# The last feature pair of each FFN chunk: third operand difference from the first, split in two steps, with priority in the schedule

## The chip, the cores and the metric

One core of a Trainium2 chip. The metric is the device time of one execution in microseconds (us). Several executions are timed, and the median is compared.

## The reference

One step of a decoder layer on 512 new prompt tokens and 8 sample tokens (520 columns), model width 1024: half a SwiGLU FFN, a mixer (causal pooling beside a Mamba-2 state-space scan), half a second SwiGLU FFN, a final norm. The change touches the two FFNs alone:

```python
def _swiglu(x, wg, wu, wd):
    return (jax.nn.silu(x @ wg) * (x @ wu)) @ wd

h = h + 0.5 * _swiglu(_rms_norm(h, ffn1_norm[l]), ffn1_w_gate[l], ffn1_w_up[l], ffn1_w_down[l])
```

The inner width is 2816, which is 22 tiles of 128, called features here. All inputs are float32.

## The kernel before

**Arithmetic.** A float32 product is emulated: each operand is split into a high part (a rounded cast, ScalarE) and a low part (operand minus high part, VectorE), and `mm3` (L122 to L127) issues three matmuls, high by high (L123), high weight by low activation (L126), low weight by high activation (L127), each 128x128 by 128x260. 260 is half of the 520 tokens.

**Seven products instead of eight.** Gate and up weights of a feature (or two output tiles `d`, `d + 1` of the down projection), two halves of the contraction and two token halves make a 2x2 by 2x2 block product. The class `Ffn` does it with seven products of blocks (`product`, L412 to L439), whose operands are sums and differences of blocks. For the down projection the activation side comes from *pairs* of features: `gx` is the first one's output and `go` the second one's, each with two token halves, and `xd` are four differences of them. The seven operands of a pair lie as slots of one tile `gt` (high parts 0 to 6, low parts 7 to 13): slot 0 is `gx0`, 1 `go0`, 2 `go1`, 3 to 6 `xd0` to `xd3`. Products use them so: product 1 slot 0, product 2 slot 1, product 5 slot 3, product 6 slot 5, product 3 slot 2, product 7 slot 4, product 4 slot 6.

**PSUM.** Products 1, 6, 7 and 4 accumulate one after another in one bank `A`; 5 and then 3 in the second half of `BE`; 2 in its first half. After products 1, 6, 7 and 5 ScalarE copies the bank out (`ac`, L437) before the next product may go on in it. So product 6 waits for the copy of product 1, product 7 for that of 6, product 4 for that of 7, and product 3 for that of 5.

**Weights.** `load` splits for each step the weight blocks `whi/wlo_..a` (products 1 and 2), `shi/slo_..c` (made from the sum `s1`; products 7 and 5), `shi/slo_..d` (from `s2`; products 6 and 3) and `whi/wlo_..b` (product 4). The high parts are ScalarE casts (L107). The low parts come from VectorE (L114), or for half of `wlo` from an ScalarE negation (L110) and an accumulating DMA that GpSimd issues (L111). The tag `shi` has two buffers, `whi` three.

**Loops.** The features go in chunks of 6, 6, 6 and 4; the first three chunks are paired. `rest` runs for each paired chunk the steps of its features, then the step of the next chunk's first feature, then four down steps `(c, d)`, d = 0, 2, 4, 6. In the profile `A1d`, `BE1d`, `shi_1d_0c` and so on are those of ffn1's down steps (2d: ffn2), here of chunk 0. A `step` opens product 1, then flushes the pending step before it (its product 4 and `close`), then runs products 5, 6, 3, 7, 2 and the element-wise `gates`. Each of a down step's products reads three pairs (three times three matmuls); the chunk's last pair is finished last: its second feature's half 1 is known after `gates`, half 0 only after that feature's product 4, in `close`. `g_split` makes the operands: for the last pair in two calls, one in `gates` (`late=False`) and one in `close` (`late=True`).

**What sets the order.** The source order above is only the start: a list scheduler with a timeline model places the instructions of all engines, moving matmuls of different steps past one another where data and buffers allow it, by priorities that follow the source. `tc.high_priority()` around a block raises the priority of its instructions. On the chip each engine takes its instructions in the order that results.

The places that the change touches are the boundaries "last feature of a paired chunk, first feature of the next, first down step": feature 5 with 6, 11 with 12, 17 with 18, in both FFNs, six in all.

Of the kernel before, what the change touches and what calls it, by code (L numbers as in the profile page):

```python
# [11 lines left out]
AF = mybir.ActivationFunctionType  # L12
ALU = mybir.AluOpType
# [8 lines left out]
HB = NT // 2  # L22
# [12 lines left out]
PAIRED = 3  # L35
# [26 lines left out]
def tile_trunk_step(ctx: ExitStack, tc: tile.TileContext, ins: dict, outs: dict):  # L62
    nc = tc.nc
# [144 lines left out]
    class Ffn:  # L208
# [42 lines left out]
        def g_split(self, f, late=None):  # L251
            role = self.role(f)
            if role == "plain" and late is not False:
                self.g_plain(f, self.out[f])
            if role != "second":
                return
            last = f == self.chunks[self.chunk[f]][-1]
            if not last and late is False:
                return
            gx, go = self.gx, self.out[f]  # L260
            if not last or late is not True:
                self.gt[f] = (self.gp.tile([P, 14, HB], F32R, tag="gt", bufs=3, name=f"gt{self.i}_{f}"),
                              self.gp.tile([P, 4, HB], F32, tag="xd", name=f"gd{self.i}_{f}"))
            t, xd = self.gt[f]

            def low(x, q):
                hi, lo = t[:, 0:7][:, q], t[:, 7:14][:, q]
                nc.scalar.copy(hi, x)
                nc.vector.tensor_tensor(out=lo, in0=x, in1=hi.bitcast(F32), op=ALU.subtract)

            if not last or late is not True:
                nc.vector.tensor_tensor(out=xd[:, 0], in0=gx[:, 0], in1=gx[:, 1], op=ALU.subtract)
                nc.vector.tensor_tensor(out=xd[:, 1], in0=go[:, 1], in1=gx[:, 1], op=ALU.subtract)
                nc.vector.scalar_tensor_tensor(out=xd[:, 2], in0=xd[:, 1], scalar=-1.0, in1=gx[:, 0], op0=ALU.mult,
                                               op1=ALU.subtract)
                low(gx[:, 0], 0)
                if last:
                    low(go[:, 1], 2)
                    low(xd[:, 0:3], slice(3, 6))
            if last and late is False:  # L280
                return
            nc.vector.scalar_tensor_tensor(out=xd[:, 3], in0=xd[:, 2], scalar=-1.0, in1=go[:, 0], op0=ALU.mult,
                                           op1=ALU.subtract)
            if last:
                low(go[:, 0], 1)
                low(xd[:, 3], 6)
            else:
                low(go, slice(1, 3))
                low(xd, slice(3, 7))
# [154 lines left out]
        def gates(self, k):  # L444
            n = f"{self.i}_{k}" if not isinstance(k, tuple) else f"{self.i}d{k[1]}_{k[0]}"
            r = self.nx[3].rearrange("p (b t) -> p b t", b=2)
            tg = self.tg[k] = self.wx.tile([P, 2, HB], F32, tag="tg", bufs=2, name=f"tg{n}")
            a, c = self.ac[k]
            nc.vector.tensor_tensor(out=tg, in0=self.BE[k][:, :, :HB], in1=a, op=ALU.add)  # L449
            if isinstance(k, tuple):  # L450
                hd, hn = h[:, k[1]], h[:, k[1] + 1, HALVES[1]]
                nc.vector.tensor_tensor(out=hd, in0=hd, in1=tg.rearrange("p b t -> p (b t)"), op=ALU.add)
                nc.vector.tensor_tensor(out=hn, in0=hn, in1=c[:, 0], op=ALU.subtract)
                return
            nc.vector.tensor_tensor(out=tg, in0=tg, in1=r, op=ALU.mult)  # L455
            nc.scalar.activation(out=tg, in_=tg, func=AF.Silu)  # L456
            self.g_homes(k)
            nc.vector.tensor_tensor(out=tg, in0=tg, in1=r, op=ALU.mult)  # L458
            self.up(k, 1, c[:, 0])
            self.g_split(k, False)  # L460

        def up(self, k, b, u):
            out, tg = self.out[k][:, b], self.tg[k][:, b]
# [2 lines left out]
        def close(self, k):  # L466
            if isinstance(k, tuple):
                hn = h[:, k[1] + 1, HALVES[0]]
                nc.vector.tensor_tensor(out=hn, in0=hn, in1=self.A[k][:, :HB], op=ALU.subtract)
                return  # L470
            self.up(k, 0, self.A[k][:, :HB])
            self.g_split(k, True)

        def scales(self):
            return rstds(self.nx, f"f{self.i}")
# [821 lines left out]
```

## Time and profile before

| | |
|---|---|
| median of 3 executions | 982.45 us (980.93 to 982.63) |
| the profiled execution | 982.63 us, its span 980.9 us |
| mean granted TensorE clock | 0.995 |
| matmuls (PE) busy | 950.7 us, 97% |
| VectorE (DVE) busy | 876.8 us, 89% |
| ScalarE (ACT) busy | 682.9 us, 70% |
| GpSimd (POOL) busy | 220.3 us, 22% |

The span is from the first to the last instruction of the profiled execution; 1.7 us of its time lie outside. Busy times are sums over an engine's instructions as the profiler recorded them. A matmul is listed with some 0.28 us from start to end, but matmuls are pipelined: what a stretch costs is read from start to start. Where a row ends in brackets, the engine was idle for that long before the instruction, and the name is what released it.

### The profile page before, as it was taken

Reading aid. Unit: us, or ns where it says so; the run is one execution under the profiler, and the core shown is the slowest. Engines: PE = TensorE matmul, PEld = TensorE weight load, DVE = VectorE, ACT = ScalarE, POOL = GpSimd, SP = SyncE. Lnnn points to the kernel's source line nnn. Section 1 sums busy time; section 2 is a strip of 40 time slices with the busy share of each in tenths; the row PEclk is TensorE's granted clock in tenths of the full one; section 3 lists DMA queues with packets and bytes.
Section 4 is the critical chain, followed back from the end, with each engine's and each line's share of the span. In section 5 each row is a group of like instructions: output and inputs, shape, how many; then the busy total and the mean of one; then the engine's idle time right before and its main releaser. Section 6 shows DMA issues by size and latency. Waiting matters only on the chain.

```text
span 980.9 us, 20300 instructions
## 1 busy us (share of the span) xinstructions
PE 950.7 (97%) x7660; PEld 928.2 (95%) x7660; DVE 876.8 (89%) x1624; ACT 682.9 (70%) x1267; POOL 220.3 (22%) x321
## 2 busy tenths in 40 slices
PE   7999999999999999999999999999999999999996
PEld 6999999999999999999899998899999999999995
DVE  7999899989988698688979987999999998999976
ACT  8777777777777565694754335678888888887864
POOL 0111211221121000167311000113343233233300
PEclk9999999999999999999999999999999999999998
DMA  7666766576566242363334333357687768767732
GB/s 244 179 145 141 184 141 161 128 183 165 120 158 162 78 159 87 103 210 92 120 98 164 100 110 94 106 149 165 165 215 184 183 157 223 191 155 190 190 91 88
DMA packets 63858, 146.51 MB, mean 149 GB/s; under 512 B 9288, under 2 KB 22536, under 8 KB 63760
## 3 DMA queue, kind: packets, MB, share of 16 engines
q1 hardware_dynamic: 41168, 103.78, 33.3%
q0 software_dynamic: 22592, 41.43, 23.3%
q8 instruction: 60, 0.98, 0.4%
q14 instruction: 38, 0.31, 0.1%
HBM read 137.85 MB, written 7.34 MB: 148 GB/s over the span
## 4 chain that ended last, share of the span: by engine, by line
PE 82%; DVE 9%; ACT 3%; DMA 3%; issue 2%; SPq 0%; POOL 0%; DVEq 0%; ACTq 0%
PE A L127 7%; PE A L123 7%; PE A L126 7%; PE BE L123 6%; PE BE L126 6%; PE BE L127 6%; PE P L315 3%; PE wo L123 2%; PE wo L127 2%; PE wo L126 2%; PE inz L123 2%; PE inz L126 2%; PE inz L127 2%; PE A2d L126 2%; PE A2d L127 2%
## 5 line engine op out<-in xcount | busy, mean ns | idle before, releaser
L437 ACT COPY ac<-A 128x260 f32<-128x260 f32 x123 | 45.3, 370 | 19.5 <-PE A L127 19.2
L385 DVE TENSOR_TENSOR s<-raw 128x1024 f32<-128x1024 f32 x41 | 49.9, 1217 | 2.0 <-DMA raw<-in_w2gu 0.9
L107 ACT CAST whi_wo<-raw_wo 128x1024 fp32r<-128x1024 f32 x12 | 12.6, 1046 | 36.8 <-issue 10.3
L1005 POOL DMA_DIRECT2D out_nss<-hs x32 | 20.8, 649 | 76.8 <-DVE hs L1023 76.8
L126 PE MATMUL wo<-catg,whi_wo 128*128 128x260 f32 x128 | 36.4, 285 | 1.3 <-DVE catg L1154 1.3
L123 PE MATMUL wo<-catg,whi_wo 128*128 128x260 f32 x128 | 37.3, 292 | 0.3 <-DVE h L1123 0.3
L123 PE MATMUL inz<-xh_mx,whi_inz 128*128 128x260 f32 x128 | 37.5, 293 | 0.0
L315 PE MATMUL P<-xg_f,raw 128*128 128x260 f32 x128 | 31.7, 401 | 5.5 <-ACT sq_f L163 5.5
L126 PE MATMUL inz<-xl_mx,whi_inz 128*128 128x260 f32 x128 | 36.9, 288 | 0.0
L127 PE MATMUL inz<-xh_mx,wlo_inz 128*128 128x260 f32 x128 | 36.9, 288 | 0.0
L123 PE MATMUL inx<-xh_mx,whi_inx 128*128 128x260 f32 x128 | 36.4, 285 | 0.0
L127 PE MATMUL wo<-catg,wlo_wo 128*128 128x260 f32 x128 | 36.4, 285 | 0.0
L127 PE MATMUL inx<-xh_mx,wlo_inx 128*128 128x260 f32 x128 | 36.2, 283 | 0.0
L126 PE MATMUL inx<-xl_mx,whi_inx 128*128 128x260 f32 x128 | 36.1, 282 | 0.0
L315 PEld LDWEIGHTS P<-xg_f,raw 128*128 128x128 f32 x128 | 25.2, 201 | 9.3 <-ACT xg_f L192 5.5
L449 DVE TENSOR_TENSOR tg<-BE,ac 128x520 f32<-128x520 f32 x41 | 28.4, 693 | 5.5 <-PE BE L127 5.5
L869 DVE SCALAR_TENSOR_TENSOR A<-U,h,A 128x544 f32<-128x544 f32 x36 | 29.0, 805 | 4.0 <-ACT A L867 3.2
L458 DVE TENSOR_TENSOR tg<-tg,r_f 128x520 f32<-128x520 f32 x41 | 28.4, 694 | 1.2 <-ACT tg L456 1.0
L455 DVE TENSOR_TENSOR tg<-tg,r_f 128x520 f32<-128x520 f32 x41 | 28.4, 693 | 0.1
L386 DVE TENSOR_TENSOR s<-s,raw 128x512 f32<-128x512 f32 x41 | 28.0, 683 | 0.0
L387 DVE TENSOR_TENSOR s<-s,raw 128x512 f32<-128x512 f32 x41 | 28.0, 682 | 0.0
L456 ACT ACTIVATE tg<-tg 128x520 f32<-128x520 f32 x41 | 26.1, 638 | 2.5 <-DVE tg L455 2.2
(1798 smaller groups left out, 4788.2 us busy)
## 6 DMA issues: line engine op xcount, KB each, us to landing
raw<-in_w2gu SPq DMA_DIRECT2D x44, 512.0 KB, 4.9
raw<-in_w1gu SPq DMA_DIRECT2D x42, 512.0 KB, 4.7
raw_1d<-in_w1d SPq DMA_DIRECT2D x24, 384.0 KB, 4.0
raw_2d<-in_w2d SPq DMA_DIRECT2D x24, 384.0 KB, 4.2
raw_wo<-in_w_out SPq DMA_DIRECT2D x12, 512.0 KB, 4.3
ab<-scr_acs SPq DMA_DIRECT2D x8, 512.0 KB, 4.1
h<-in_state_ssm SPq DMA_DIRECT2D x16, 256.0 KB, 3.7
raw_inz<-in_w_in SPq DMA_DIRECT2D x8, 512.0 KB, 3.9
```

Source lines behind the costliest of these rows:

```text
L123: first = nc.tensor.matmul(ps, whi, xhi, start=start, stop=False, **kw)
L126: nc.tensor.matmul(ps, whi, xlo, start=False, stop=False, **kw)
L127: nc.tensor.matmul(ps, wlo, xhi, start=False, stop=stop, **kw)
L315: nc.tensor.matmul(self.banks[f, u][b][:, :HB], ws(self.raw[f][:, u], j + 4 * q), xg[:, slot[q]], start=j == q == 0, stop=j == 3 and q == ...
L385: nc.vector.tensor_tensor(out=s1, in0=diag, in1=up0, op=ALU.add)
L386: nc.vector.tensor_tensor(out=s2[:, 0], in0=s1[:, 1], in1=raw[:, 0, :nb], op=ALU.add)
L387: nc.vector.tensor_tensor(out=s2[:, 1], in0=s2[:, 0], in1=raw[:, 0, nb : 2 * nb], op=ALU.add)
L437: nc.scalar.copy(keep, out[:, :HB])
L449: nc.vector.tensor_tensor(out=tg, in0=self.BE[k][:, :, :HB], in1=a, op=ALU.add)
L455: nc.vector.tensor_tensor(out=tg, in0=tg, in1=r, op=ALU.mult)
L458: nc.vector.tensor_tensor(out=tg, in0=tg, in1=r, op=ALU.mult)
L869: nc.vector.scalar_tensor_tensor(out=A[:, :n], in0=U[:, j : j + n], scalar=w(j), in1=A[:, :n], op0=ALU.mult, op1=ALU.add)
```

## The change

Three edits in the class `Ffn`. First, the difference `xd2`, for all pairs, is made as `-xd0 - go1` instead of `-xd1 - gx0` (both are `gx1 - gx0 - go1`). Second, for the last pair of a chunk, the operands split in the early call are `gx0`, then `xd0` alone (slot 3), then `xd1` and `xd2` together (slots 4 and 5), then `go1` (slot 2); before, they were `gx0`, `go1`, and `xd0` to `xd2` together (slots 3 to 5). Third, a helper `first_if` puts the rest of `gates` (from the scaling on) and `close` of that last feature under high priority.

```diff
                 nc.vector.tensor_tensor(out=xd[:, 1], in0=go[:, 1], in1=gx[:, 1], op=ALU.subtract)
-                nc.vector.scalar_tensor_tensor(out=xd[:, 2], in0=xd[:, 1], scalar=-1.0, in1=gx[:, 0], op0=ALU.mult,
+                nc.vector.scalar_tensor_tensor(out=xd[:, 2], in0=xd[:, 0], scalar=-1.0, in1=go[:, 1], op0=ALU.mult,
                                                op1=ALU.subtract)
                 low(gx[:, 0], 0)
                 if last:
+                    low(xd[:, 0], 3)
+                    low(xd[:, 1:3], slice(4, 6))
                     low(go[:, 1], 2)
-                    low(xd[:, 0:3], slice(3, 6))
...
-            nc.vector.tensor_tensor(out=tg, in0=tg, in1=r, op=ALU.mult)
-            nc.scalar.activation(out=tg, in_=tg, func=AF.Silu)
-            self.g_homes(k)
-            nc.vector.tensor_tensor(out=tg, in0=tg, in1=r, op=ALU.mult)
-            self.up(k, 1, c[:, 0])
-            self.g_split(k, False)
+            with self.first_if(k):
+                nc.vector.tensor_tensor(out=tg, in0=tg, in1=r, op=ALU.mult)
+                nc.scalar.activation(out=tg, in_=tg, func=AF.Silu)
+                self.g_homes(k)
+                nc.vector.tensor_tensor(out=tg, in0=tg, in1=r, op=ALU.mult)
+                self.up(k, 1, c[:, 0])
+                self.g_split(k, False)
+
+        def first_if(self, k):
+            c = self.chunk[k]
+            return tc.high_priority() if c < PAIRED and k == self.chunks[c][-1] else nullcontext()
...
-            self.up(k, 0, self.A[k][:, :HB])
-            self.g_split(k, True)
+            with self.first_if(k):
+                self.up(k, 0, self.A[k][:, :HB])
+                self.g_split(k, True)
```

## The prediction

> **What bounds the kernel now.** I read the page first (busy times, then the chain of work that ended last), then the view of what TensorE waited for, then the timeline of PE and ACT at the places that this view names.
>
> ```profile
> span 980.9 us, 20300 instructions
> ...
> PE 950.7 (97%) x7660; PEld 928.2 (95%) x7660; DVE 876.8 (89%) x1624; ACT 682.9 (70%) x1267; POOL 220.3 (22%) x321
> ...
> PE 82%; DVE 9%; ACT 3%; DMA 3%; issue 2%; SPq 0%; POOL 0%; DVEq 0%; ACTq 0%
> ```
>
> PE is busy for 97% of the span, so at most 30 us could be won by any reordering, and only at the places where PE stands still. The changed code feeds the first step of each down projection of a paired chunk (six of these, "1d" in ffn1 and "2d" in ffn2). There PE waits like this (us in total, times, longest):
>
> ```profile
> PE BE2d L126 <- DVE gt L269: 1.7, 2, 0.9
> ...
> PE BE1d L126 <- DVE gt L269: 0.9, 3, 0.3
> PE BE1d L123 <- ACT ac1d L437: 0.8, 3, 0.3
> ```
>
> Two kinds: product 5 waits for the low half of the last pair's differences (L269), and product 3, which goes on in product 5's bank, waits for the copy of product 5 (L437). The timeline of PE at the first of the six shows the price of each (columns: start, duration, instruction, idle before and releaser).
>
> ```profile
> 88.65 0.28 PE L123 MATMUL A1d<-gt,shi_1d_0d 128*128 128x260 f32 x1
> 89.22 0.39 PE L126 MATMUL BE1d<-gt,shi_1d_0c 128*128 128x260 f32 x1 [0.29 <-DVE gt L269]
> ...
> 89.68 0.28 PE L127 MATMUL A1d<-gt,slo_1d_0d 128*128 128x260 f32 x1
> 90.25 0.39 PE L123 MATMUL BE1d<-gt,shi_1d_0d 128*128 128x260 f32 x1 [0.29 <-ACT ac1d L437]
> ...
> 92.29 0.28 PE L126 MATMUL BE1d<-gt,whi_1d_0a 128*128 128x260 f32 x1
> 92.41 0.28 PE L127 MATMUL BE1d<-gt,wlo_1d_0a 128*128 128x260 f32 x1
> 92.53 0.28 PE L123 MATMUL A1d<-gt,shi_1d_0c 128*128 128x260 f32 x1
> ```
>
> The steady spacing from start to start is 0.12 us (92.29, 92.41, 92.53). 88.65 to 89.22 is 0.57, a loss of 0.45; 89.68 to 90.25 loses 0.45 again. The matmul behind a waiting one also comes late, by about 0.10 (below, 691.36 to 691.58 is 0.22). So this boundary loses 2 x (0.45 + 0.10) = 1.1 us, and the waits view, with three waits of each kind of at most 0.3, says that ffn1's three are alike. In ffn2:
>
> ```profile
> 701.76 0.28 PE L127 MATMUL A2d<-gt,slo_2d_0d 128*128 128x260 f32 x1
> 702.76 0.39 PE L123 MATMUL BE2d<-gt,shi_2d_0d 128*128 128x260 f32 x1 [0.71 <-ACT ac2d L437]
> ```
> ```profile
> 793.34 0.28 PE L123 MATMUL A2d<-gt,shi_2d_1d 128*128 128x260 f32 x1
> 794.48 0.39 PE L126 MATMUL BE2d<-gt,shi_2d_1c 128*128 128x260 f32 x1 [0.85 <-DVE gt L269]
> ```
> ```profile
> 794.95 0.28 PE L127 MATMUL A2d<-gt,slo_2d_1d 128*128 128x260 f32 x1
> 795.51 0.39 PE L123 MATMUL BE2d<-gt,shi_2d_1d 128*128 128x260 f32 x1 [0.29 <-ACT ac2d L437]
> ```
>
> Chunk 0 loses 1.00 - 0.12 + 0.10 = 1.0. Chunk 1 loses 1.02 + 0.44 + 0.20 = 1.7, and the waits view (1.7 us in two L269 waits) puts chunk 2 at the same. All six: 3 x 1.1 + 1.0 + 2 x 1.7 = **7.7 us**. This is all that the change can take away at these places.
>
> **The change, part by part.** *Arithmetic.* The third difference needs only the first difference and the second feature's token half 1, instead of the second difference and the first feature. Same operation, same width: nothing by itself.
>
> *The 780-wide split becomes 260 and 520.* Per boundary one more ACT cast and one more DVE subtract, of 260.
>
> ```profile
> 88.21 0.96 DVE L269 TENSOR_TENSOR gt<-gd,gt 128x780 fp32r<-128x780 f32 x1
> ```
> ```profile
> L269 DVE TENSOR_TENSOR gt<-gx,gt x18: 415/419/426, 38.9 to 873.8; 128x260 fp32r<-128x260 f32 x18
> ```
>
> By these rows a subtract takes 0.42 at 260 and 0.96 at 780, so 0.27 for each 260 more and 0.15 that doesn't depend on the width; the split adds 6 x 0.15 = 0.9 us of DVE time. I cost it at nothing: the first difference's pieces are made in the stretch where PE still works at the next chunk's first feature, and the 520-wide rest is needed only at product 6's end (below). Without that cover it would be 0.9.
>
> The Trainium skill, "VectorE: DVE Perf Modes", section "The TRN2 errata", speaks against such splitting: an operation from SBUF pays a fixed cost each time, so small tiles pay it per tile. Its formula for an fp32 add, (N+151)/0.96 ns, makes 0.43 at 260 and 0.97 at 780, by estimate; the rows agree, and if DVE set the end the sum would be 0.9 higher.
>
> *Priority and order.* This is the part that matters. The scheduler puts the changed kernel's instructions on PE in another order at all six boundaries: (1) product 5 runs to its end, last pair included, ahead of product 4 of the next chunk's first feature; so the L269 wait and, as the copy then has 12 matmuls (1.4 us) to be made in, the L437 wait both go: -7.7 us. (2) Product 6's last two matmuls (L126 and L127 on the last pair's slot 5, whose low half now comes with the 520-wide subtract) go behind all of products 3 and 2. Right behind them stand the first two matmuls of the *next* down step's product 5, which use `shi_..c` of that step; only then comes product 7. That cast takes the buffer of this step's `shi_..d`, whose last reader is now the moved L126 of product 6. So PE, which takes its matmuls in order, must wait there for a cast that can't start before a matmul two places ahead. Before, the last reader was product 3, long before the cast was needed:
>
> ```profile
> 89.82 0.38 ACT L437 COPY ac1d<-BE1d 128x260 f32<-128x260 f32 x1 [0.67 <-PE BE1d L127]
> 90.09 0.38 ACT L437 COPY ac1d<-A1d 128x260 f32<-128x260 f32 x1
> 91.52 0.83 ACT L107 CAST shi_1d_0c<-s_1d 128x768 fp32r<-128x768 f32 x1 [1.05 <-PE BE1d L126]
> 92.61 0.52 ACT L107 CAST whi_1d_0b<-raw_1d 128x384 fp32r<-128x384 f32 x1 [0.25 <-PE BE1d L126]
> 93.03 0.52 ACT L110 ACTIVATE wlo_1d_0b<-raw_1d 128x384 fp32r<-128x384 f32 x1
> ```
>
> On ACT the changed order is `whi_..b`, `wlo_..b`, then the shi cast, then product 6's copy. From the start of product 2's last L126 (92.29 above): 0.32 to `whi_..b` (92.61), 0.42 to `wlo_..b` (93.03), 0.42 to the shi cast (same width before it), 0.83 for the cast, 0.05 to PE (89.82 + 0.38 = 90.20, PE at 90.25): 2.04 us. PE would have been there four matmuls on, at 0.48. The loss is 1.56 + 0.10 for the one behind = **1.66 us per boundary**. Product 7 follows at 2.04 + 0.22 + 0.12 = 2.38 and needs product 6's copy, which is made right behind the cast: at the latest at 1.16 + 0.83 + 0.38 = 2.37, just in time.
>
> The lower bound of this stall is an ACT that stands free when product 6's L126 has started: 0.32 + 0.83 + 0.05 - 0.24 + 0.10 = 1.06. As upper bound I take one more copy ahead of the cast and the product-6 copy late by the same: 1.66 + 0.27 (89.82 to 90.09) + 0.10 = 2.0. I take 1.66, since ACT's order is known.
>
> The Trainium skill, "ScalarE: Activation LUTs", section "Rules for kernel authors", budgets 0.3 us and 0.83 ns per element for an activation: 0.62 at 384 and 0.94 at 768, by estimate. By it the stall would be 2.2 and the sum 3 us higher; the rows (0.83, and 0.42 from start to start) are shorter and decide.
>
> *Two features of ffn2, chunk 0.* The priorities also change the order in there:
>
> ```profile
> 690.81 0.28 PE L126 MATMUL A<-xtl_f,shi_6d 128*128 128x260 f32 x1
> 691.36 0.39 PE L123 MATMUL BE<-xth_f,shi_6d 128*128 128x260 f32 x1 [0.27 <-ACT ac L437]
> 691.58 0.28 PE L126 MATMUL BE<-xtl_f,shi_6d 128*128 128x260 f32 x1
> 691.84 0.39 PE L127 MATMUL A<-xth_f,slo_6d 128*128 128x260 f32 x1
> ```
>
> At feature 6, product 5 now comes ahead of product 4 and its copy ahead of a weight cast; this loss goes: 0.43 + 0.10 + 0.14 + 0.11 = -0.78. At feature 2 it goes the other way: product 4 of feature 4 now stands ahead of product 5, whose copy stands on ACT behind two operations of the next feature.
>
> ```profile
> 670.50 0.28 PE L126 MATMUL BE<-xtl_f,shi_2d 128*128 128x260 f32 x1
> 670.85 0.39 PE L127 MATMUL A<-xth_f,slo_2d 128*128 128x260 f32 x1
> ```
> ```profile
> 670.22 1.05 ACT L107 CAST whi_5a<-raw 128x1024 fp32r<-128x1024 f32 x1 [0.90 <-PE A L126]
> 671.18 0.63 ACT L110 ACTIVATE wlo_5a<-raw 128x512 fp32r<-128x512 f32 x1
> ```
>
> `whi_5a` is released 10 matmuls (1.2 us) earlier, at 669.02; `wlo_5a` follows at 669.98 (0.96 on), the copy at about 670.53 and ends at 670.91; product 3 starts at 670.96 instead of 670.38. That loses 0.58 + 0.10 = 0.68, and replaces the present wait for `slo_2d` (0.35 - 0.12 + 0.10 = 0.33): +0.35.
>
> POOL's order around ffn2's first chunks moves too (its weight DMAs against stores of the state); SP's loads keep theirs. POOL is busy for 22%, so I put 0, with -0.5 to +2 us as bounds (the longest wait of a PE row above, 0.9, twice).
>
> **Sum.** -7.7 + 6 x 1.66 - 0.78 + 0.35 = **+1.8 us**. The profiled execution took 982.63 us (span 980.9 and 1.7 around it), so 984.4; the median before is 0.18 lower, hence 984.3 as forecast for the median. With 1.06 per stall the sum is -1.8 (980.7), with 2.0 it is +3.9 (986.4); POOL's bounds on top make 980 to 988.
>
> **Rivals.** *A: both old waits go and no new one comes,* because the low half of slot 5 is ready and the shi cast finds its buffer free: -7.7 - 0.8 + 0.3 = -8.2, so 974.3; half of it is 978.4. For it: ACT idles 1.05 and 0.25 us right there, so it has room. Against: the cast is released by a matmul two places ahead of its own reader, and not even a free ACT brings that under 1.06.
>
> *B: slower by more, DVE.* The subtracts put ahead push back what stood there: the low weights `slo_..d` and the half-1 additions of the next step arrive late, and PE waits after product 7 as well. DVE is busy for 89% and gives way from the point where it lags PE; the delay is one subtract of 0.42 and the following matmul's 0.10 per boundary, six times: +3.1, in all +4.9, so 987.2. Against: the new stall itself hands DVE 1.66 us just ahead of that.
>
> *C: nothing visible.* PE's stalls exchange one for one, the time stays at 982.4 +/- 1. For it: 1.66 against 1.7 in ffn2's chunks 1 and 2; against: ffn1 has only 1.1 to give back.
>
> **Chances.** Forecast (983 to 986) 0.45, B 0.2, A or a good half of it 0.2, C 0.15. A measurement of this kernel can tell about 0.2% (1.96 us) from no change, so "faster" ends at 980.5 and "slower" begins at 984.4. The forecast lies at that line; with its upper bounds longer than its lower ones I give two thirds of it to slower: 0.3 + 0.2 = 0.5; same 0.15 + 0.15 = 0.3; faster 0.2. The range reaches half way into A and over B: 978 to 988; the forecast's own is 983 to 986.
>
> **What would show it.** In the profile after: no "BE1d L126 <- DVE gt L269" and hardly any "BE1d L123 <- ACT ac1d" in PE's waits; in their place six waits of BE1d/BE2d L123 on the cast `shi_..c` (L107), each with a gap of about 1.7 us from start to start; feature 6 of ffn2 without its wait, feature 2 with one on the copy. The prediction is wrong if these shi waits are under 1 us, if product 7 waits long for product 6's copy, or if new waits on `slo` or POOL's `wlo` show.

## The result, and the profile after

The changed kernel takes 984.89 us (median of 13 executions, 983.49 to 986.89) against 982.63 us for the kernel before in the same series (13 executions, 980.93 to 985.72). The ratio is 1.0026, with a 95% interval of 1.0018 to 1.0034: slower by about 2.3 us, where 1.8 was forecast.

The page of the profiled execution of the changed kernel (986.0 us):

```profile
span 984.2 us, 20310 instructions
...
PE 948.9 (96%) x7660; PEld 927.1 (94%) x7660; DVE 877.3 (89%) x1630; ACT 681.6 (69%) x1273; POOL 219.1 (22%) x321
...
PE 83%; DVE 8%; ACT 3%; DMA 3%; issue 2%; POOL 0%; SPq 0%; DVEq 0%; ACTq 0%
```

PE does the same 7660 matmuls, and the span is 3.3 us longer. Its busy time is 1.8 us shorter, most of it because the profiled execution of the kernel before had a dip of the clock (last section); so it stands still for 5.1 us more (984.2 - 948.9 = 35.3 against 980.9 - 950.7 = 30.2). The view of what PE waited for says where (us in total, times, longest):

```profile
PE BE1d L123 <- ACT shi_1d_0c L107: 1.4, 1, 1.4
PE BE1d L123 <- ACT shi_1d_1c L107: 1.4, 1, 1.4
PE BE1d L123 <- ACT shi_1d_2c L107: 1.4, 1, 1.4
...
PE BE2d L123 <- ACT shi_2d_2c L107: 1.4, 1, 1.4
PE BE2d L123 <- ACT shi_2d_0c L107: 1.4, 1, 1.4
PE BE2d L123 <- ACT shi_2d_1c L107: 1.4, 1, 1.4
```

No row "BE1d L126 <- DVE gt L269" or "BE1d L123 <- ACT ac1d" is left, nor their partners of ffn2. All of the old waits went, and six equal new ones came. The first of them on PE's timeline:

```profile
91.48 0.28 PE L126 MATMUL BE1d<-gt,whi_1d_0a 128*128 128x260 f32 x1
...
91.72 0.28 PE L126 MATMUL A1d<-gt,shi_1d_0d 128*128 128x260 f32 x1
91.84 0.28 PE L127 MATMUL A1d<-gt,slo_1d_0d 128*128 128x260 f32 x1
93.51 0.39 PE L123 MATMUL BE1d<-gt,shi_1d_0c 128*128 128x260 f32 x1 [1.39 <-ACT shi_1d_0c L107]
93.73 0.28 PE L126 MATMUL BE1d<-gt,shi_1d_0c 128*128 128x260 f32 x1
93.85 0.32 PE L123 MATMUL A1d<-gt,shi_1d_0c 128*128 128x260 f32 x1
```

and ScalarE beside it:

```profile
91.80 0.51 ACT L107 CAST whi_1d_0b<-raw_1d 128x384 fp32r<-128x384 f32 x1 [1.22 <-PE BE1d L126]
92.21 0.52 ACT L110 ACTIVATE wlo_1d_0b<-raw_1d 128x384 fp32r<-128x384 f32 x1
92.64 0.81 ACT L107 CAST shi_1d_0c<-s_1d 128x768 fp32r<-128x768 f32 x1
93.36 0.36 ACT L438 COPY ac1d<-A1d 128x260 f32<-128x260 f32 x1
```

Product 2's last L126 starts at 91.48; `whi b` starts 0.32 later, `wlo b` 0.41 after that, the cast another 0.43 later; the cast is 0.81 long, and PE goes on at 93.51. From 91.84 to 93.51 are 1.67 us where 0.12 is normal, and the next comes 0.10 late: 1.65 us lost. All six places show the same 1.67 from start to start.

And the data for which product 6's tail was put off had been there for long. VectorE (the first of the two operations in this row is the 520-wide one) and PE:

```profile
89.09 1.03 DVE L269 TENSOR_TENSOR gt<-gd,gt 128x520 fp32r<-128x520 f32 x2
```
```profile
89.67 0.28 PE L123 MATMUL A1d<-gt,shi_1d_0d 128*128 128x260 f32 x1
```

The 520-wide subtract takes 0.69 where it stands alone, as in ffn2:

```profile
703.45 0.69 DVE L269 TENSOR_TENSOR gt<-gd,gt 128x520 fp32r<-128x520 f32 x1
```

So it ends at 89.78 here, just after PE has started product 6's L123 on the last pair. The L126 behind it could have started at about 89.8; it starts at 91.72, after products 3 and 2.

### The profile page after: what moved, and what is told of

Same layout as the page of the kernel before. It is cut to its first block, busy times and chain, and to the rows that moved or that the text cites. A ratio compares the mean times of both kernels' runs of the same rounds, so it can differ in the third digit from the quotient of the medians.

```text
span 984.2 us, 20310 instructions
## 1 busy us (share of the span) xinstructions
PE 948.9 (96%) x7660; PEld 927.1 (94%) x7660; DVE 877.3 (89%) x1630; ACT 681.6 (69%) x1273; POOL 219.1 (22%) x321
## 4 chain that ended last, share of the span: by engine, by line
PE 83%; DVE 8%; ACT 3%; DMA 3%; issue 2%; POOL 0%; SPq 0%; DVEq 0%; ACTq 0%
PE A L127 8%; PE A L123 7%; PE A L126 7%; PE BE L127 6%; PE BE L126 6%; PE BE L123 6%; PE P L316 3%; PE wo L123 2%; PE wo L126 2%; PE wo L127 2%; PE A2d L126 2%; PE A2d L123 2%; PE A2d L127 2%; PE A1d L123 2%; PE A1d L127 2%
## 5 line engine op out<-in xcount | busy, mean ns | idle before, releaser
L126 PE MATMUL wo<-catg,whi_wo 128*128 128x260 f32 x128 | 36.4, 285 | 1.3 <-DVE catg L1161 1.3
L123 PE MATMUL wo<-catg,whi_wo 128*128 128x260 f32 x128 | 37.3, 292 | 0.3 <-DVE h L1130 0.3
L123 PE MATMUL inz<-xh_mx,whi_inz 128*128 128x260 f32 x128 | 36.8, 287 | 0.0
L123 PE MATMUL inx<-xh_mx,whi_inx 128*128 128x260 f32 x128 | 36.4, 285 | 0.0
L126 PE MATMUL inz<-xl_mx,whi_inz 128*128 128x260 f32 x128 | 36.2, 282 | 0.0
L126 PE MATMUL inx<-xl_mx,whi_inx 128*128 128x260 f32 x128 | 36.1, 282 | 0.0
```

Source lines behind the costliest of these rows:

```text
L123: first = nc.tensor.matmul(ps, whi, xhi, start=start, stop=False, **kw)
L126: nc.tensor.matmul(ps, whi, xlo, start=False, stop=False, **kw)
```

## The experiments

Each ratio is to the kernel before, timed in the same series on the same chip. Theory A throughout: the cost is that product 6's tail stands too late, and the cast and the copy on ScalarE can only follow it. The rivals are named with the runs.

**Formula and split without the priority.**

```diff
-            return tc.high_priority() if c < PAIRED and k == self.chunks[c][-1] else nullcontext()
+            return nullcontext()
```

> The changed kernel without its third edit (no high priority); formula and separate split stay. Theory A: the separate split alone moves product 6's last two matmuls behind product 2, and the priority only swaps a few vector operations; then the six waits of 1.4 us for the cast of shi c stay as they are and the time is that of the changed kernel, 984.9, within 1 us. Rival B (as the prediction had it): the priority moves the matmuls; then the shi waits are gone and the time is 982.6 or below.

Measured: 987.35 us (6 executions, 984.71 to 989.75; ratio 1.0049, 1.0030 to 1.0067). The median misses the expected 984.9 by 2.5, and its size says little: three of the six lie at 984.7 to 985.7, three at 989.0 to 989.8 with a granted clock of 0.993, and why those are longer stays open. The waits decide, here the first of each FFN:

```profile
PE BE1d L123 <- ACT shi_1d_0c L107: 1.4, 1, 1.4
...
PE BE2d L123 <- ACT shi_2d_0c L107: 1.4, 1, 1.4
```

All six are there without any priority. Rival B falls. In fact every engine but VectorE has its instructions in the same order as in the changed kernel; the priority swaps six pairs of neighbours on VectorE.

**The priority alone.** The old formula and the old 780-wide split, under `first_if`.

> The kernel before with the third edit alone: high priority, old formula, old 780-wide split. Theory A: no shi wait; the waits for the 780-wide low half (L269) and for product 5's copy stay at 7.7 us in all, the time is that of before, 982.6, within 1 us. Rival B: the priority brings the six shi waits of 1.4 and the time goes to 984 to 986.

Measured: 984.35 us, ratio 1.0013 (1.0002 to 1.0023). No wait for shi; the old waits stay, and one grows:

```profile
PE BE1d L126 <- DVE gt L269: 2.0, 3, 0.7
...
PE BE1d L123 <- ACT ac1d L437: 0.8, 3, 0.3
```

The L269 wait in ffn1 was 0.9 before. So the priority doesn't bring the new stall, and by itself it costs about 1.2 us (0.13%), a little beyond what theory A allowed for.

**The separate split alone.**

```diff
                 if last:
+                    low(xd[:, 0], 3)
+                    low(xd[:, 1:3], slice(4, 6))
                     low(go[:, 1], 2)
-                    low(xd[:, 0:3], slice(3, 6))
```

> The kernel before with the second edit alone: slot 3 by itself, slots 4 and 5 together. Theory A: what a boundary costs depends on where product 6's tail stands and on how many matmuls lie between it and the first reader of the next shi cast. In ffn1 nine matmuls of the next product 1 now lie there: 2.04 us less 0.48 less 1.08 leaves 0.5 and 0.1 for the next, 0.6 per boundary instead of 1.66. In ffn2 chunk 0 product 6 isn't split up: 0. Chunks 1 and 2 as in the changed kernel, 1.66 each. Sum 3 x 0.6 + 0 + 2 x 1.66 = 5.1 instead of 7.7: about 980 to 981, if features elsewhere cost no more than before. Rival C (the boundaries cost the same wherever the tail stands, because ACT is what is late): 984 to 985.

Measured: 981.22 us, ratio 0.9986 (0.9978 to 0.9995), faster than before. Product 6's tail is put off in five of six places, so this edit is what moves it. But only two of the five have the full stall. In ffn1, nine matmuls of the next product 1 stand behind the tail, and they first wait themselves, for the bank that the next feature's output `gx` still has to be read from:

```profile
PE BE2d L123 <- ACT shi_2d_1c L107: 1.4, 1, 1.4
PE BE2d L123 <- ACT shi_2d_2c L107: 1.4, 1, 1.4
...
PE A1d L123 <- DVE gx L465: 1.1, 3, 0.4
```

The first of them, from product 6's tail to the first reader of the next cast:

```profile
91.00 0.28 PE L126 MATMUL A1d<-gt,shi_1d_0d 128*128 128x260 f32 x1
91.12 0.28 PE L127 MATMUL A1d<-gt,slo_1d_0d 128*128 128x260 f32 x1
91.78 0.36 PE L123 MATMUL A1d<-gt,whi_1d_0a 128*128 128x260 f32 x1 [0.38 <-DVE gx L465]
...
92.92 0.28 PE L123 MATMUL BE1d<-gt,shi_1d_0c 128*128 128x260 f32 x1
```

That costs 0.54 + 0.08, the 0.6 that was worked out, but the wait is another one: the cast ends at 92.74, just ahead of its reader, because PE has lost that time already. ffn2's chunk 0, where product 6's tail is not put off, has no wait at all, as expected. Rival C, ScalarE late wherever the tail stands, falls.

**The formula alone.**

```diff
-                nc.vector.scalar_tensor_tensor(out=xd[:, 2], in0=xd[:, 1], scalar=-1.0, in1=gx[:, 0], op0=ALU.mult,
+                nc.vector.scalar_tensor_tensor(out=xd[:, 2], in0=xd[:, 0], scalar=-1.0, in1=go[:, 1], op0=ALU.mult,
```

> The kernel before with the first edit alone: the third difference from the first, the 780-wide split kept, no priority. Theory A (the separate split moves product 6's tail; the formula moves only features 2, 4 and 6 of ffn2): no wait for the shi cast; the wait for the 780-wide low half (L269) stays at all six boundaries, in ffn1 the wait for product 5's copy goes because seven matmuls of product 6 now stand between; feature 6's wait of 0.8 goes and feature 2's grows to about 1.1. Sum 3 x -0.5 + 0.2: 981 to 982. Rival D (the formula is what moves the tail): six shi waits, 984 to 986.

Measured: 982.89 us, ratio 0.9994 (0.9983 to 1.0006): no difference, and above the expected 981 to 982. No shi wait, so rival D falls. The old waits remain in ffn2 only:

```profile
PE BE2d L126 <- DVE gt L269: 2.4, 3, 0.8
...
PE BE2d L123 <- ACT ac2d L437: 0.8, 3, 0.3
```

In ffn1 both are gone, more than expected. ffn2 gives that back: all three chunks now wait for L269 (2.4 us in all, 1.7 before), and feature 16 waits for `slo_16d` (0.5 us). What feature 6 gains, feature 2 loses. The order at features 2, 4 and 6 is that of the changed kernel: that part comes from the formula.

These runs together show something that none shows alone. The formula by itself changes nothing in the time, the split by itself makes the kernel faster, and the two together (the run without priority) have the changed kernel's order and all six stalls: 984.7 at the least, where the split alone took 982.84 at the most. The split puts the tail off; with the formula it is put off in ffn2's chunk 0 too, and in ffn1 the next product 5 stands behind it in place of product 1. So four of the six full stalls need both.

**Product 6's tail back ahead of product 2.** The changed kernel with two order constraints and nothing else. In this and the next diffs `f` is a product's first matmul, `self.ends` holds the last matmul of each step's product, and `no_sync` stands for a dependency that fixes the order on the engine and adds no semaphore:

```diff
+                if isinstance(k, tuple) and k[1] == 0 and p == 2 and j == 0:
+                    tc.add_manual_dep(f.ins, self.ends[k, 6].ins.name, no_sync, reason="order")
+                if isinstance(k, tuple) and k[1] == 0 and p == 4 and j == 0:
+                    tc.add_manual_dep(f.ins, self.ends[(k[0], 2), 1].ins.name, no_sync, reason="order")
```

> The changed kernel with two order constraints in each paired chunk's first down step: product 2 not before the end of product 6, product 4 not before the next step's product 1. Nothing else. Theory A: product 6's tail now ends 11 matmuls (1.32 us) ahead of the first reader of the next shi cast, and the cast needs 0.32 + 0.83 + 0.05 = 1.20; product 7's copy is ready at 1.5 of 1.56. All six stalls go and no old one returns: 984.9 - 6 x 1.65 = 975 to 976. Rival C (ACT or VectorE is late there anyway): waits of half a us or more on the cast, the copy or slo remain at most boundaries, 979 or more.

Measured: 980.09 us, ratio 0.9967 (0.9955 to 0.9979). All six shi waits are gone, and no copy of a down step is waited for; the cast does what the arithmetic said. But the time is not 975. The constraints move other products, and small waits stand where there was none, for `gx` and `slo`:

```profile
PE A2d L123 <- DVE gx L478: 0.6, 3, 0.2
...
PE A2d L127 <- DVE slo_2d_2d L114: 0.2, 1, 0.2
PE A2d L127 <- DVE slo_2d_1d L114: 0.2, 1, 0.2
```

With the late matmul behind each wait, and gaps of 0.25 for which no releaser is shown in ffn1, start to start they add up to about 3.4 us in the FFNs. The expectation had put them at zero. With them the 975 becomes 978.4; the kernel before is 0.5 slower in this series (983.13), and the last 1.2 us stay open (the wait for `catp`, below, is 1.5 longer in this profile than in that of the kernel before).

**The two matmuls in front of product 7 taken away.** The changed kernel, in which the next step's product 5 may not start before this step's product 7 has ended:

```diff
+                if isinstance(k, tuple) and k[1] == 2 and p == 5 and j == 0:
+                    tc.add_manual_dep(f.ins, self.ends[(k[0], 0), 7].ins.name, no_sync, reason="order")
```

> The changed kernel with one order constraint: the next step's product 5 not before the end of this step's product 7, so that the two matmuls that wait for the shi cast no longer stand ahead of product 7. Theory A (product 6's tail is late, and what is behind it on ScalarE in the order whi b, wlo b, shi cast, copy is late with it): product 7 now waits itself, for product 6's copy, which comes behind the cast: 1.16 + 0.74 + 0.38 + 0.05 = 2.33 less 0.48, and 0.1: 1.95 per boundary instead of 1.65, so 1.8 slower than the changed kernel, 986 to 987. Rival E (the two matmuls in front of product 7 are the fault): product 7 waits 0.5 at most, 978 to 979.

Measured: 988.32 us (6 executions, ratio 1.0049, 1.0033 to 1.0065), above the expected 986 to 987. The interval touches that of the changed kernel and holds the ratio of the run without priority, so again the waits decide. Product 7 now waits for the copy:

```profile
PE A1d L123 <- ACT ac1d L443: 5.0, 3, 1.7
PE A2d L123 <- ACT ac2d L443: 5.0, 3, 1.7
```

1.7 each instead of 1.4, the 0.3 more that theory A asked for (from start to start each place loses 1.92; 1.95 was worked out). The two matmuls are not the fault: whatever stands behind product 6's tail waits, because ScalarE takes `whi b`, `wlo b` and the cast first.

**Product 6 in one piece.** The changed kernel, product 3 not before the end of product 6:

```diff
+                if isinstance(k, tuple) and k[1] == 0 and p == 3 and j == 0:
+                    tc.add_manual_dep(f.ins, self.ends[k, 6].ins.name, no_sync, reason="order")
```

> The changed kernel with one order constraint: product 3 of the first down step not before the end of product 6, so product 6 is not torn apart at all. Theory A: its L126 on the last pair then waits for the 520-wide low half, which by the changed kernel's rows ends at 89.78 in ffn1 (the slot is 89.55: 0.3 and 0.1) and at 704.14 in ffn2 (slot 703.58: 0.6 and 0.1): 3 x 0.4 + 3 x 0.7 = 3.3 us instead of 9.9, 978 to 979. Rival C (ScalarE or VectorE late anyway): the shi cast or the copy is waited for all the same, 982 or more.

Measured: 979.97 us, ratio 0.9965 (0.9951 to 0.9979), 1 us above the expectation and the lowest of all, level with p6_in_place. What product 6 waits for now is the 520-wide low half. The waits view lists it for ffn2:

```profile
PE A2d L126 <- DVE gt L269: 1.3, 3, 0.4
```

From start to start the first of these is:

```profile
698.25 0.28 PE L123 MATMUL A2d<-gt,shi_2d_0d 128*128 128x260 f32 x1
698.95 0.39 PE L126 MATMUL A2d<-gt,shi_2d_0d 128*128 128x260 f32 x1 [0.43 <-DVE gt L269]
699.18 0.28 PE L127 MATMUL A2d<-gt,slo_2d_0d 128*128 128x260 f32 x1
```

That is 0.58 + 0.11 lost, as worked out (0.6 and 0.1). In ffn1 the same matmul comes 0.29 late (88.71 to 89.12) and the next 0.10, again as worked out, though no releaser is shown. Two matmuls of ffn2 that wait for `slo` add about 1 us, which the expectation did not have. So a loss of at most 0.7 us for the data was dodged at the price of 1.65.

**The split and the two constraints, without formula and priority.** The diffs of "The separate split alone" and of the two constraints, on the kernel before.

> The kernel before with the separate split alone, and the two order constraints of the run p6_in_place. Theory A: formula and priority add nothing; ffn1's boundaries cost 0.3 each, ffn2's chunk 0 nothing, chunks 1 and 2 about 1.0 each with the slo waits that p6_in_place showed: 2.9 instead of 7.7, 978 to 979, at or below p6_in_place. Rival: the formula is needed for the early low half, then L269 waits come back, 981 or more.

Measured: 980.88 us, ratio 0.9976 (0.9959 to 0.9993). The early low half doesn't need the formula: no L269 wait comes back. The time is above the expected 979, and whether it differs from p6_in_place is unclear, as the intervals overlap. The profile names a copy in ffn1 and one `slo` far from the boundaries that no other run shows:

```profile
PE BE1d L123 <- ACT ac1d L446: 1.2, 3, 0.4
PE A L127 <- DVE slo_15d L114: 1.1, 1, 1.1
```

## Why the prediction was right, and where it was not

**The old waits, 7.7 us:** right. All of them are gone from the changed kernel.

**The new stall, 1.66 us six times:** right, 1.65 measured, and each piece of it within 0.02 us (0.32, 0.41, 0.43, 0.81 against 0.32, 0.42, 0.42, 0.83). Product 7 follows 2.37 us after product 2's last L126 (91.48 to 93.85), 2.38 was worked out. The budget of the Trainium skill, "ScalarE: Activation LUTs", section "Rules for kernel authors" (0.3 us and 0.83 ns per element), is too high for these casts: 0.51 at 384 and 0.81 at 768 here, so the slope nearly agrees (0.78 ns) and the fixed part is about 0.2; back to back it is only 0.1.

**What causes it:** wrong. The prediction put the new order under "priority and order" and the split at nothing. The runs show that the separate split alone moves product 6's tail (five of six places), that the formula alone moves features 2, 4 and 6 and, together with the split, brings four of the six full stalls, and that the priority moves no matmul once both are there. The step that failed is that the new order was credited to the priority, with the formula put at nothing by itself and the split counted by its VectorE time alone. That the split costs nothing there agrees with the busy time (877.3 us against 876.8). Why the scheduler holds the two matmuls back is not on record; that its timeline has the split's second part later than it came on the chip is a guess.

**Feature 6 of ffn2, -0.78:** right, its wait is gone. **Feature 2, +0.35:** the term that was mis-sized. PE after, and the two engines that release it:

```profile
672.14 0.28 PE L126 MATMUL A<-xtl_f,shi_2d 128*128 128x260 f32 x1
672.79 0.39 PE L123 MATMUL BE<-xth_f,shi_2d 128*128 128x260 f32 x1 [0.37 <-ACT ac L438]
673.02 0.28 PE L126 MATMUL BE<-xtl_f,shi_2d 128*128 128x260 f32 x1
673.52 0.39 PE L127 MATMUL A<-xth_f,slo_2d 128*128 128x260 f32 x1 [0.23 <-DVE slo_2d L114]
```
```profile
671.85 0.63 ACT L110 ACTIVATE wlo_5a<-raw 128x512 fp32r<-128x512 f32 x1
672.38 0.36 ACT L438 COPY ac<-BE 128x260 f32<-128x260 f32 x1
```
```profile
670.17 1.21 DVE L386 TENSOR_TENSOR s<-raw 128x1024 f32<-128x1024 f32 x1
...
672.25 1.21 DVE L114 TENSOR_TENSOR slo_2d<-s,shi_2d 128x1024 fp32r<-128x1024 f32 x1
```

The copy behind `wlo_5a` costs 0.53 + 0.11, as worked out (0.68). But the prediction let this wait replace the one for `slo_2d`; VectorE makes `slo_2d` behind a sum of the next feature (1.21) and two shorter operations, and PE waits for it too: 0.38 + 0.11 more. The term is +0.79 instead of +0.35.

**What the sum left out:** In the profiled execution feature 16 also waits for its `slo` (0.55 us), but not in the run without priority, whose matmuls stand in the same order, so this isn't steady. Boundaries and features together are 1.65 x 6 - 7.7 - 0.78 + 0.79 = +2.2 us, against 2.26 between the medians. That the two meet within 0.1 us is partly luck: the interval of the ratio allows 1.8 to 3.3, and the wait of feature 16 and those under "What stays open" are not in the sum.

**The rivals.** A (no new wait) and C (nothing visible) did not happen. B, VectorE late behind product 7, did not show at the boundaries. By the prediction's own signs one spoke against it: new waits on `slo` do show (`slo_2d` and `slo_16d`, 0.2 and 0.3 us in the waits view), at features and not behind product 7. The 987.2 given for B is a slip, 984.3 + 3.1 is 987.4. That POOL's changed order costs nothing agrees with PE's waits, in which no POOL row stands.

**What stays open:** PE's wait for `catp` in the mixer, between the FFNs, was 0.7 before, 1.5 in the changed kernel and between 0.7 and 2.2 in the experiments. The changed kernel without its two front matmuls has 0.7, so the change needn't be the cause; it was not tried by itself.

## What to carry to other kernels

When an operation is split so that its first part comes earlier, a list scheduler may put off the work that needs its second part, as it did here in five of six places. Look at what the put-off work holds: here two matmuls of 0.12 us kept a weight buffer and an accumulator from being released, and a loss of at most 0.7 us was traded for one of 1.65 us. When a change brings a new order, build each edit alone and in pairs and compare the orders before naming a cause (here the split alone was faster, and with the formula it was slower), and hold the order where it matters with a constraint: that turned +0.26% into -0.35%.

## What the runs showed of the hardware

The granted clock fell to about half for some 3.4 us in the middle of three of the ten profiled executions (the kernel before, the priority alone, product 6's tail back ahead), each time in the mixer. One window of the kernel before and the matching one of the changed kernel (stretch, its length, busy time of PE, PEld, DVE, ACT and POOL, clock, DMA share, GB/s):

```profile
473.40:477.10 3.70, 3.70 (x21) 3.70 (x20) 3.70 (x8) 2.63 (x9) 1.96 (x2) 0.54 0.50 145
```
```profile
475.10:479.00 3.90, 3.39 (x26) 3.16 (x27) 3.90 (x7) 3.73 (x10) 3.09 (x3) 1.00 0.59 174
```

Inside the dip matmuls start every 0.22 us (474.15, 474.37, 474.58) instead of 0.12, and it cost the kernel before about 1.5 us in its profiled execution (18 matmul starts took 3.69 us, from 473.41 to 477.10, where 2.16 is normal). Each dip came behind a stretch in which PE had little to do: it was busy for 1.73 of the 3.40 us before it in the kernel before (470.20 to 473.60), 1.55 and 1.22 in the other two. The changed kernel was as idle there (1.38 of 3.40, 473.00 to 476.40) and did not dip, so the idle stretch alone doesn't decide. The 1.5 us are two thirds of the effect under study, so the profiled times (986.0 and 982.63) alone could not have told how much the change costs; the medians and the single waits could.
